# Hybrid encoder trunk: convolution steps moved between the scores and the transpositions of the prompt's second pair of heads

## Chip, cores and metric

One NeuronCore of a Trainium2 chip runs the whole program. The metric is the device time in microseconds (us) of one execution, as the median of several runs. The engines are TensorE (PE in the profile, its weight loads PEld), VectorE (DVE), ScalarE (ACT), GpSimd (POOL) and SyncE (SP), which here only issues DMAs.

## What is computed

Two batches pass through one layer with the same weights: a prompt of 256 tokens and a sample of 512, so six tiles of 128 tokens, 1024 features each. The layer is

```python
h = rmsnorm(x, norm1)
gq, gk, gv, gg, glr, dq, dk, dvv, sz, sxbc, sdt = split(h @ w_in)
x = x + concat([gla(...), diff(...), ssd(...)]) @ w_out
x = x + square(relu(rmsnorm(x, norm2) @ w_mlp1)) @ w_mlp2
```

Two of the three mixers matter here. Differential attention (diff) has four heads, each with two maps: q and k are normed over 64 features and partly rotated, and with p the softmax of the scaled scores the output is (p1 - lam p2) v, normed again. The state-space mixer (ssd) first sends 768 channels through a convolution of five taps along the tokens and silu; 512 of them are its x, 128 each its B and C:

```python
xbc = silu(conv(sxbc, conv_w, width=5) + conv_b)
```

## The kernel before

**Work and order.** The program is written in Python as one long function. A scheduler then sets the order on each engine's queue, by the dependences, by priorities and by its own idea of how long things take. `tc.high_priority()` moves what stands in it ahead in that order; `tc.issue_after(i)` keeps what stands in it behind the instruction i. On the chip each engine works its queue strictly in the order written, TensorE too, so what stands at the head and waits holds all behind it.

**Products.** All weights are float32 and are split into a high part (a rounding, ScalarE's cast, L135) and a low part (VectorE's subtraction, L136), `wh` and `wl`; a product is three matmuls (`mm3`, L97 to L101). A unit of weights is 256 columns of w_in: two loads `wr` of 512 KB, two casts, two subtractions. `wh` and `wl` have two buffers each, so a unit's cast waits for the last product of the unit before the previous one. `tm_steps` multiplies tokens by a unit (tile `tm`, 256 columns, 48 matmuls for two token tiles); `fm_unit` (L201) makes features by tokens (tile `fm`, 384 columns, 24 matmuls for one of two halves). Both, and the convolution's transpositions `xtmp`, share three accumulators of PSUM (`acc`, N_ACC = 3); all else shares the other five (`mx`).

**Norms of q and k.** `diff_in(p)` (L801) makes q and k of head pair p in two units. After each two token tiles ScalarE copies the product to `dqk` and squares it to `dsq`; VectorE sums (L817, `dss`), POOL takes the power -1/2 (`rstd_of`, L160, `drs`), VectorE scales (L819) and rotates (L824 to L827); a DMA writes `dqk` to memory. The small columns come from `small`, a ring of eight tiles of 32 columns.

**Heads.** `diff_head(p, h, 0)` (L841) reads q, k and v of one prompt head back, transposes q and k (`qT`, L866), splits them (`qs`, `ks`, `kz`), and for each of the two query tiles makes the two maps' scores (`sc`, L890 and L891), the row maximum (`dmx`, L892), the exponential with its sum (`pr`, L893), mixes the maps (`dratio`, `pr`, L894 to L896), transposes the result (`wT`, L899) and splits it (`wt`, L903 and L904). After both tiles it multiplies by v (`O`) and norms (`ss`, `ors`, `dg`, `rb`). It yields after its set-up and after each tile; `take_turns` lets the heads of a pair advance in turn.

**Convolution.** `ssd_conv` (L616) takes three units of 256 channels, in the order 2, 0, 1, and in each two times 128 channels. For each it makes both halves of the product, ScalarE copies them to `xp` (L625 to L628) and starts the sum (`zh`, L632), VectorE adds four taps (L634). `tail`, always one channel group late, does the silu (tanh on ScalarE, L199; VectorE L646 or L654), and for x transposes the result back (`xtmp`, L650; `xt`, L651).

**The stretch in question.** Behind the first mixer (gla), at about 222 us of the trace, the program has:

```python
for p in range(2):
    diff_in(p)
    take_turns(*(diff_head(p, h, 0) for h in range(2)))
xt, bcm = [None] * 4, [None] * 2
tail = ssd_conv((2, 0, 1), xt, bcm)
ssd_gate(0)
tail()
btm = ssd_btm(bcm[0])
```

`ssd_gate` makes the gate's tokens (`tm`, `sz`), `ssd_btm` transposes B (`btmp`). `er` and `ar` are the tables of decays of `ssd_chunk` (L726 to L729), which the scheduler also places in this stretch. Behind it come the states and chunks of the prompt's ssd, w_out and the MLP of the prompt with the sample's heads among them, and the MLP of the sample.

Of the kernel before, what the change touches and what calls it, by code (L numbers as in the profile page):

```python
# [11 lines left out]
F32 = mybir.dt.float32  # L12
# [31 lines left out]
def hybrid_kernel(ctx, tc, io):  # L44
# [12 lines left out]
    def nm(s):  # L57
        uid[0] += 1
        return f"{s}_{uid[0]}"
# [17 lines left out]
    d2 = tag(first, "d2", 2, 2 * (T + 32))  # L77

    def small(name, n):
        return sm.tile([P, 32], F32, tag="sm", name=nm(name))[:, :n]  # L80

    def small2(name, n):
        return sm.tile([P, 32], F32, tag="sm2", name=nm(name), bufs=3)[:, :n]

    def acc(name):
        return psa.tile([P, 512], F32, tag="acc", name=nm(name))
# [7 lines left out]
    def bc(ap, shape):  # L94
        return ap.to_broadcast(shape)

    def mm3(out, l, r, first, last):  # L97
        (lh, ll), (rh, rl) = l, r
        mm(out, lhsT=lh, rhs=rh, start=first, stop=False)  # L99
        mm(out, lhsT=lh, rhs=rl, start=False, stop=False)  # L100
        return mm(out, lhsT=ll, rhs=rh, start=False, stop=last).ins  # L101
# [55 lines left out]
    def rstd_of(out, ss, n, scale, small=small):  # L157
        ms = small("ms", n)
        dve.tensor_scalar(ms, ss, scale, EPS, op0=ALU.mult, op1=ALU.add)
        pool.tensor_tensor(out, ms, nhalf[:, :n], ALU.pow)  # L160
# [40 lines left out]
    def fm_unit(w, c, m, consume, parts):  # L201

        for ops, o, n, d in parts:
            ps = acc("fm")
            for k in range(KT):
                mm3(ps[:m, :n], (w[0][:, k, c:c + m], w[1][:, k, c:c + m]),
                    tuple(z[:, o:o + n] for z in ops[k]), k == 0, k == KT - 1)
            consume(ps[:m, :n], slice(d, d + n))

    halves_ = [(hT, 0, 384, 0), (hT, 384, 384, 384)]  # L210

# [403 lines left out]
                act.activation(decs[gs], ptb[gs, :, 4 * g:4 * g + 4, :].rearrange("p d h c -> p c d h"), AF.Exp)  # L615
        yield scr, decs, tms, ew  # L616

    def ssd_conv(us, xt, bcm):
        def conv(j):
            xp = i3("xp", n=776)  # L620

            def consume(ps, ts):
                with tc.high_priority():
                    if ts.start == 0:
                        act.copy(xp[:, 2:258], ps[:, 0:256])  # L625
                        act.copy(xp[:, 262:390], ps[:, 256:384])
                        return
                    act.copy(xp[:, 390:774], ps)  # L628
                for a in (0, 258, 774):
                    pool.memset(xp[:, a:a + (4 if a == 258 else 2)], 0.0)  # L630
                zh = i3("zh", n=772)
                act.activation(zh, xp[:, 0:772], AF.Identity, scale=half[:, j:j + 1], bias=half[:, 30 + j:31 + j])  # L632
                for k in range(1, 5):
                    dve.scalar_tensor_tensor(zh, xp[:, k:k + 772], half[:, 6 * k + j:6 * k + j + 1], zh,  # L634
                                             op0=ALU.mult, op1=ALU.add)
                tails.append((j, xp, zh))
            return consume

        tails = []

        def tail():
            j, xp, zh = tails.pop(0)
            tanh(xp[:, 0:772], zh, 1.0)
            if j < 4:
                xt[j] = v128(i3("xt"))
                dve.scalar_tensor_tensor(zh, xp[:, 0:772], 1.0, zh, op0=ALU.add, op1=ALU.mult)  # L646
                for (a, b) in SEQS:
                    pt = acc("xtmp")
                    for c in range(a, b):
                        nc.tensor.transpose(pt[:, (c - a) * P:(c - a + 1) * P], zh[:, off(c):off(c) + P], ident)  # L650
                    act.copy(xt[j][:, a:b, :], v128(pt[:, :(b - a) * P]))  # L651
            else:
                bcm[j - 4] = i3("bcm", n=772)
                dve.scalar_tensor_tensor(bcm[j - 4], xp[:, 0:772], 1.0, zh, op0=ALU.add, op1=ALU.mult)  # L654

        for u in us:
            w = in_unit(C_SX + 256 * u)
            for i in range(2):
                fm_unit(w, i * P, P, conv(2 * u + i), halves_)
                if len(tails) > 1:  # L660
                    tail()
        return tail

    def ssd_btm(bfm):
        btm = s2("btm")
# [20 lines left out]
    def hd(ap):  # L686
        return ap.rearrange("p (h d) -> p h d", d=64)
# [117 lines left out]
    def diff_in(p):  # L805

        for i, c0 in ((0, C_DQ), (1, C_DK)):
            w = in_unit(c0 + 256 * p)

            def cons(ps, t0):  # L810
                q = i3("dqk", n=512)
                with tc.high_priority():
                    act.copy(q.rearrange("p (t c) -> p t c", t=2), ps)
                sq = i3("dsq", n=512)
                act.activation(sq, q, AF.Square)
                ss, rs = small("dss", 8), small("drs", 8)
                dve.tensor_reduce(ss, hd(sq), AX.X, ALU.add)  # L817
                rstd_of(rs, ss, 8, 1.0 / 64)
                dve.tensor_tensor(hd(q), hd(q), bc(rs[:, :, None], [P, 8, 64]), ALU.mult)  # L819
                q4 = q.rearrange("p (t m d) -> p t m d", t=2, m=4)  # L820
                rab = sq[:, 0:256].rearrange("p (a t m d) -> p a t m d", a=2, t=2, m=4)
                ra, rb = rab[:, 0], rab[:, 1]
                ts = slice(t0, t0 + 2)
                dve.tensor_tensor(ra, q4[:, :, :, 0:16], bc(ropeg[:, i, 0, ts, None, :], [P, 2, 4, 16]), ALU.mult)  # L824
                dve.tensor_tensor(rb[:, :, :, 0:8], q4[:, :, :, 8:16], bc(ropeg[:, i, 1, ts, None, 0:8], [P, 2, 4, 8]), ALU.mult)
                dve.tensor_tensor(rb[:, :, :, 8:16], q4[:, :, :, 0:8], bc(ropeg[:, i, 1, ts, None, 8:16], [P, 2, 4, 8]), ALU.mult)
                dve.tensor_tensor(q4[:, :, :, 0:16], ra, rb, ALU.add)  # L827
                nc.sync.dma_start(out=(dqd, dkd)[i][p][t0 // 2], in_=q.rearrange("p (t c) -> p t c", t=2))
            tm_unit(w, cons)
        for _ in v_steps[p]:  # L830
            pass
# [6 lines left out]
            nc.sync.dma_start(out=dvd[p][t0 // 2], in_=v)  # L838
        return tm_steps(lambda: in_unit(C_DV + 256 * p), vcons)

    def diff_head(p, h, s):  # L841

        a, b = SEQS[s]
        kt = b - a
# [36 lines left out]
        for pq in range(0, kt, 2):  # L881
            wts = [[tt("wt", F32R, 512).rearrange("p (k q) -> p k q", k=2) for _ in range(kt // 2)] for _ in range(2)]
            for qi in range(2):
                tq = slice((pq + qi) * P, (pq + qi + 1) * P)
                pr = cc("pr", n=2 * nk).rearrange("p (m i) -> p m i", m=2)
                mxs, ratio = small("dmx", 2), small("dratio", 1)
                sums = allsums[:, pq + qi, :]
                for m in range(2):
                    ps = mx("sc")
                    mm(ps[:, :nk], lhsT=qs[:, m, tq], rhs=ks[:, m], start=True, stop=False)  # L890
                    mm(ps[:, :nk], lhsT=qs[:, m, tq], rhs=kl[:, m], start=False, stop=True)  # L891
                    dve.tensor_reduce(mxs[:, m:m + 1], ps[:, :nk], AX.X, ALU.max, negate=True)  # L892
                    act.activation(pr[:, m], ps[:, :nk], AF.Exp, bias=mxs[:, m:m + 1], accum_out=sums[:, m:m + 1])  # L893
                dve.reciprocal(ratio, sums[:, 1:2])  # L894
                dve.scalar_tensor_tensor(ratio, ratio, nlam, sums[:, 0:1], op0=ALU.mult, op1=ALU.mult)
                dve.scalar_tensor_tensor(pr[:, 0], pr[:, 1], ratio, pr[:, 0], op0=ALU.mult, op1=ALU.add)  # L896
                ps = mx("wT")
                for k_ in range(kt):
                    nc.tensor.transpose(ps[:, k_ * P:(k_ + 1) * P], pr[:, 0, k_ * P:(k_ + 1) * P], ident)  # L899
                cols_ = slice(qi * P, (qi + 1) * P)  # L900
                for k2 in range(kt // 2):
                    src = v128(ps[:, k2 * 256:k2 * 256 + 256])
                    act.copy(wts[0][k2][:, :, cols_], src)  # L903
                    dve.tensor_tensor(wts[1][k2][:, :, cols_], src, rd(wts[0][k2][:, :, cols_]), ALU.subtract)  # L904
                yield
            for k_ in range(kt):
                mm3(po[:, pq * P:pq * P + 256], tuple(v[:, k_, :] for v in vs),
                    tuple(w[k_ // 2][:, k_ % 2, :] for w in wts), k_ == 0, k_ == kt - 1)
# [193 lines left out]
    rope = t2("rope", n=192).rearrange("p (a t d) -> p a t d", a=2, t=NT)  # L1102
    nc.sync.dma_start(out=rope, in_=io["c_rope"])

    qk16 = small("qk16", 32).rearrange("p (a d) -> p a d", a=2)
    for i, nme in enumerate(("diff_qnorm", "diff_knorm")):
        nc.sync.dma_start(out=qk16[:, i, :], in_=bc(io[nme][0:1, 0:16], [P, 16]))
    ropeg = const.tile([P, 2, 2, NT, 16], F32, name="ropeg")
# [45 lines left out]
        for m in range(2):  # L1154
            pool.memset(rd(z[64 - 64 * m:128 - 64 * m, m]), 0.0)

    for p in range(2):
        diff_in(p)
        take_turns(*(diff_head(p, h, 0) for h in range(2)))
    xt, bcm = [None] * 4, [None] * 2  # L1160
    tail = ssd_conv((2, 0, 1), xt, bcm)
    ssd_gate(0)
    tail()
    btm = ssd_btm(bcm[0])
    st = ssd_states(dt, xt, btm, *SEQS[0], tt)
    y_ops = {}
# [272 lines left out]
```

## Time and profile before

| | |
|---|---|
| runs | 1128.51, 1130.4, 1131.89 us; median 1130.4 |
| profiled execution | 1128.8 us, its span 1127.0 us |
| busy in the span: PE, PEld | 1080.3 us (96%), 982.7 us (87%) |
| busy in the span: DVE, ACT, POOL | 806.0 us (72%), 622.2 us (55%), 126.2 us (11%) |
| mean granted clock of TensorE | 0.986 |

The span is from the first to the last instruction; 1.8 us of the execution lie around it. Busy times of PE are of overlapping matmuls: one of 384 columns is shown with 0.34 us, and the next starts 0.17 us later. A wait is shown as idle time of an engine ahead of an instruction, with the instruction that ended it.

### The profile page before, as it was taken

The page shows a single profiled execution, that of the slowest core. Times are in us where ns is not written, and L with a number is a line of the kernel's source. Part 1 is how long each engine was busy: PE and PEld are TensorE (multiplying, and loading weights), DVE is VectorE, ACT ScalarE, POOL GpSimd, SP SyncE. Part 2 cuts the span into 40 slices and gives each one's busy share as a digit, 9 for nine tenths or more (in the row PEclk, how much of TensorE's full clock was granted, in tenths as well). Part 3 has the DMA queues.
Part 4 walks back from the last instruction along what each step waited for, and adds up shares of the span by engine and source line. Part 5 has one row for each costly group of instructions (what it writes and reads, how often), then busy time and mean ns, then how long its engine had stood idle before and what let it go on. Part 6 is the DMA issues. An engine that isn't in the chain of part 4 may idle for free.

```text
span 1127.0 us, 20930 instructions
## 1 busy us (share of the span) xinstructions
PE 1080.3 (96%) x8372; PEld 982.7 (87%) x8372; DVE 806.0 (72%) x1414; ACT 622.2 (55%) x1216; POOL 126.2 (11%) x184
## 2 busy tenths in 40 slices
PE   7999999999958998899999999998999999999998
PEld 7999999999958985888878897787998998998997
DVE  6579977474787578887797786857986756756752
ACT  7487584656366237656667673525553553543541
POOL 1001012120400281010101111300000000000000
PEclk9999999999989999899999999999999999999999
DMA  6212112171424354446545558642351242342312
GB/s 203 88 42 77 40 58 89 56 225 39 149 71 127 103 194 143 130 134 194 181 128 170 178 159 276 218 133 89 97 188 59 94 133 74 94 140 67 94 38 75
DMA packets 118647, 136.49 MB, mean 121 GB/s; under 512 B 8935, under 2 KB 86789, under 8 KB 118549
## 3 DMA queue, kind: packets, MB, share of 16 engines
q1 hardware_dynamic: 118517, 135.14, 37.5%
q8 instruction: 66, 1.08, 0.4%
q14 instruction: 32, 0.26, 0.1%
q10 hardware_dynamic: 32, 0.01, 0.0%
HBM read 121.44 MB, written 13.68 MB: 120 GB/s over the span
## 4 chain that ended last, share of the span: by engine, by line
PE 76%; DVE 8%; ACT 6%; DMA 5%; POOL 2%; issue 2%; SPq 0%; ACTq 0%; DVEq 0%; POOLq 0%
PE tp L100 9%; PE tp L99 9%; PE tp L101 9%; PE X L1297 7%; PE fm L99 5%; PE fm L100 5%; PE fm L101 5%; PE tm L99 4%; PE tm L101 4%; PE tm L100 4%; PE Z L1297 4%; DMA wr<-in_w_mlp 2%; DVE wl L136 2%; DMA er<-scr 2%; PE Y L1297 2%
## 5 line engine op out<-in xcount | busy, mean ns | idle before, releaser
L136 DVE TENSOR_TENSOR wl<-wr,wh 128x1024 fp32r<-128x1024 f32 x130 | 160.2, 1246 | 54.0 <-ACT wh L135 53.2
L135 ACT CAST wh<-wr 128x1024 fp32r<-128x1024 f32 x138 | 141.6, 1049 | 96.6 <-DMA wr<-in_w_mlp 49.3
L99 PE MATMUL tm<-wh,hTh 128*128 128x256 f32 x576 | 166.3, 289 | 3.6 <-ACT xp L628 3.5
L101 PE MATMUL tm<-wh,hTl 128*128 128x256 f32 x576 | 165.1, 287 | 0.0
L100 PE MATMUL tm<-wl,hTh 128*128 128x256 f32 x576 | 163.4, 284 | 0.0
L99 PEld LDWEIGHTS tm<-wh,hTh 128*128 128x128 f32 x576 | 109.9, 191 | 5.6 <-ACT xp L628 3.7
L100 PEld LDWEIGHTS tm<-wl,hTh 128*128 128x128 f32 x576 | 109.9, 191 | 0.4 <-DVE wl L136 0.2
L101 PEld LDWEIGHTS tm<-wh,hTl 128*128 128x128 f32 x576 | 110.0, 191 | 0.1
L1390 DVE TENSOR_TENSOR xres<-tp,xres 128x512 f32<-128x512 f32 x56 | 38.6, 690 | 55.4 <-PE tp L101 54.7
L99 PE MATMUL fm<-h,wh 128*128 128x256 f32 x256 | 73.0, 287 | 1.9 <-ACT relu L1002 1.9
L100 PE MATMUL fm<-h,wh 128*128 128x256 f32 x256 | 73.2, 287 | 0.0
L101 PE MATMUL fm<-h,wl 128*128 128x256 f32 x256 | 72.4, 286 | 0.5 <-DVE wl L136 0.5
L99 PE MATMUL fm<-hTh,wh 128*128 128x384 f32 x160 | 54.4, 340 | 2.2 <-ACT xp L628 2.2
L100 PE MATMUL fm<-hTl,wh 128*128 128x384 f32 x160 | 54.1, 338 | 0.0
L101 PE MATMUL fm<-hTh,wl 128*128 128x384 f32 x160 | 53.9, 337 | 0.0
L956 DVE TENSOR_TENSOR xres<-tp,xres 128x512 f32<-128x512 f32 x60 | 40.3, 683 | 17.4 <-PE tp L101 17.3
L99 PEld LDWEIGHTS fm<-h,wh 128*128 128x128 f32 x256 | 49.5, 194 | 2.6 <-ACT relu L1002 2.1
L100 PE MATMUL tp<-wl,u 128*128 128x512 f32 x128 | 50.9, 398 | 0.5 <-DVE wl L136 0.5
L101 PE MATMUL tp<-wh,u 128*128 128x512 f32 x128 | 50.6, 395 | 0.0
L99 PE MATMUL tp<-wh,u 128*128 128x512 f32 x128 | 49.8, 400 | 0.6 <-ACT wh L135 0.6
L100 PEld LDWEIGHTS fm<-h,wh 128*128 128x128 f32 x256 | 49.5, 193 | 0.6
L101 PEld LDWEIGHTS fm<-h,wl 128*128 128x128 f32 x256 | 49.3, 194 | 0.9 <-DVE wl L136 0.7
(429 smaller groups left out, 3079.9 us busy)
## 6 DMA issues: line engine op xcount, KB each, us to landing
wr<-in_w_mlp SPq DMA_DIRECT2D x100, 512.0 KB
wr<-in_w_in SPq DMA_DIRECT2D x30, 512.0 KB
wb<-in_w_mlp SPq DMA_DIRECT2D x28, 512.0 KB
wr<-in_w_out SPq DMA_DIRECT2D x24, 512.0 KB
ar<-scr SPq DMA_DIRECT2D x6, 512.0 KB
er<-scr SPq DMA_DIRECT2D x6, 512.0 KB
x<-in_x_sample SPq DMA_DIRECT2D x4, 512.0 KB
wr<-in_w_in SPq DMA_DIRECT2D x8, 256.0 KB
```

Of the source, the lines that this page charges most:

```text
L99: mm(out, lhsT=lh, rhs=rh, start=first, stop=False)
L100: mm(out, lhsT=lh, rhs=rl, start=False, stop=False)
L101: return mm(out, lhsT=ll, rhs=rh, start=False, stop=last).ins
L135: act.copy(hi, raw)
L136: dve.tensor_tensor(lo, raw, rd(hi), ALU.subtract)
L956: dve.tensor_tensor(xres[t][:, cs], ps, xres[t][:, cs], ALU.add)
L1297: mm(out, lhsT=a[l][:, k, c], rhs=b[r][:, k, :], start=first and j == k == z == 0, stop=j == 1 and k == 3 and z == 2, skip_group_check=True)
L1390: dve.tensor_tensor(xres[t][:, cs], ps, xres[t][:, cs], ALU.add)
```

## The change

Four edits.

1. `ssd_conv` becomes a generator: it yields after each half of each product, with that half's last matmul, and gets the list into which it puts its `tail`.
2. `diff_head` may be given `between`. Then, for each query tile, behind the mixing of the maps it yields, calls `between(h)`, and puts the transposition `wT` behind the instructions that this returns.
3. The program takes the first four steps of the convolution (its first unit) ahead of the second pair's heads; head 0 of that pair asks for two steps for each query tile, head 1 for one; what is left follows the heads.
4. In `diff_in` the square, the sum, the power, the scaling and the rotation stand under high priority, with a ring `small8` of nine tiles of 8 columns of their own; `small` shrinks to 16 columns, and `qk16`, its one user of 32, becomes a constant.

```diff
     def small(name, n):
-        return sm.tile([P, 32], F32, tag="sm", name=nm(name))[:, :n]
+        return sm.tile([P, 16], F32, tag="sm", name=nm(name))[:, :n]
...
+    def small8(name, n):
+        return sm.tile([P, 8], F32, tag="sm8", name=nm(name), bufs=9)[:, :n]
...
+        tails.append(tail)
         for u in us:
             w = in_unit(C_SX + 256 * u)
             for i in range(2):
-                fm_unit(w, i * P, P, conv(2 * u + i), halves_)
-                if len(tails) > 1:
+                consume = conv(2 * u + i)
+                yield fm_unit(w, i * P, P, consume, halves_[:1])
+                last = fm_unit(w, i * P, P, consume, halves_[1:])
+                if len(waiting) > 1:
                     tail()
-        return tail
+                yield last
...
-                act.activation(sq, q, AF.Square)
-                ss, rs = small("dss", 8), small("drs", 8)
-                dve.tensor_reduce(ss, hd(sq), AX.X, ALU.add)
-                rstd_of(rs, ss, 8, 1.0 / 64)
-                dve.tensor_tensor(hd(q), hd(q), bc(rs[:, :, None], [P, 8, 64]), ALU.mult)
+                ss, rs = small8("dss", 8), small8("drs", 8)
...
+                with tc.high_priority():
+                    act.activation(sq, q, AF.Square)
+                    dve.tensor_reduce(ss, hd(sq), AX.X, ALU.add)
+                    rstd_of(rs, ss, 8, 1.0 / 64, small8)
+                    dve.tensor_tensor(hd(q), hd(q), bc(rs[:, :, None], [P, 8, 64]), ALU.mult)
...
-                ps = mx("wT")
-                for k_ in range(kt):
-                    nc.tensor.transpose(ps[:, k_ * P:(k_ + 1) * P], pr[:, 0, k_ * P:(k_ + 1) * P], ident)
+                with ExitStack() as order:
+                    if between is not None:
+                        yield
+                        for last in between(h):
+                            order.enter_context(tc.issue_after(last))
+                    ps = mx("wT")
+                    for k_ in range(kt):
+                        nc.tensor.transpose(ps[:, k_ * P:(k_ + 1) * P], pr[:, 0, k_ * P:(k_ + 1) * P], ident)
...
-    for p in range(2):
-        diff_in(p)
-        take_turns(*(diff_head(p, h, 0) for h in range(2)))
-    xt, bcm = [None] * 4, [None] * 2
-    tail = ssd_conv((2, 0, 1), xt, bcm)
+    xt, bcm, tails = [None] * 4, [None] * 2, []
+    steps = ssd_conv((2, 0, 1), xt, bcm, tails)
+    diff_in(0)
+    take_turns(*(diff_head(0, h, 0) for h in range(2)))
+    diff_in(1)
+    for _ in range(4):
+        next(steps)
+    take_turns(*(diff_head(1, h, 0, lambda h: [next(steps) for _ in range(2 - h)]) for h in range(2)))
+    for _ in steps:
+        pass
     ssd_gate(0)
-    tail()
+    tails[0]()
```

What the scheduler makes of it is seen in the queues. Line numbers of the changed program are some 3 to 20 higher. **TensorE, at the first wT of the second pair, before:** `fm` are convolution products, `sc_530` and `sc_531` the scores of head 0, `sc_540` and `sc_541` those of head 1.

```order
L101 MATMUL fm_591_4718<-hTh_24_137,wl_581_4615 128x384
L890 MATMUL sc_531_4347<-ks_511_4290,qs_510_4289 128x256
L891 MATMUL sc_531_4347<-kz0_3254,qs_510_4289 128x256
L899 MATMUL wT_532_4355<-ident_94,pr_527_4339 128x128 x2
L890 MATMUL sc_540_4367<-ks_520_4318,qs_519_4317 128x256
L891 MATMUL sc_540_4367<-kz1_3258,qs_519_4317 128x256
L890 MATMUL sc_541_4372<-ks_520_4318,qs_519_4317 128x256
L891 MATMUL sc_541_4372<-kz1_3258,qs_519_4317 128x256
L650 MATMUL xtmp_594_4756<-ident_94,zh_587_4681 128x128 x2
```

**The same place in the change,** the last rows ahead of wT and the first behind it; `sc_552`, the last score of head 1, stands 29 rows ahead of wT.

```order
L102 MATMUL fm_576_4660<-hTh_24_137,wh_553_4514 128x384
L103 MATMUL fm_576_4660<-hTl_25_138,wh_553_4514 128x384
L104 MATMUL fm_576_4660<-hTh_24_137,wl_554_4515 128x384
L914 MATMUL wT_562_4590<-ident_94,pr_539_4478 128x128 x2
L655 MATMUL xtmp_579_4698<-ident_94,zh_560_4581 128x128 x2
L655 MATMUL xtmp_580_4702<-ident_94,zh_560_4581 128x128 x4
L102 MATMUL fm_586_4719<-hTh_10_123,wh_581_4708 128x384
```

Both heads' scores now stand ahead of the first wT, with the whole of `fm_576` and four rows of `fm_564` between, and the transpositions `xtmp` directly behind it.

**VectorE, the end of the same wait, in the change** (`wl_614` is the low part of the gate's weights):

```order
L904 RECIPROCAL dratio_541_4480<-dsum_536_4475 128x1
L902 TENSOR_REDUCE dmx_549_4499<-sc_551_4501 128x1
L902 TENSOR_REDUCE dmx_549_4499<-sc_552_4506 128x1
L639 SCALAR_TENSOR_TENSOR zh_560_4581<-xp_557_4524,half_644,zh_560_4581 128x772
L905 SCALAR_TENSOR_TENSOR dratio_541_4480<-dratio_541_4480,nlam_812,dsum_536_4475 128x1
L639 SCALAR_TENSOR_TENSOR zh_560_4581<-xp_557_4524,half_644,zh_560_4581 128x772
L906 SCALAR_TENSOR_TENSOR pr_539_4478<-pr_539_4478,dratio_541_4480 128x256
L139 TENSOR_TENSOR wl_614_4929<-wr_615_4930,wh_613_4928 128x1024
L139 TENSOR_TENSOR wl_614_4929<-wr_616_4934,wh_613_4928 128x1024
L651 SCALAR_TENSOR_TENSOR zh_560_4581<-xp_557_4524,zh_560_4581 128x772
```

Before, the two `wl` of the same weights stood ahead of pr; now they stand between pr and the last step of the `zh` that `xtmp_579` transposes.

**VectorE, one step of the first pair's heads, in the change** (`dqk_471` is a normed tile of the second pair's q):

```order
L902 TENSOR_REDUCE dmx_431_3759<-sc_434_3766 128x1
L832 TENSOR_TENSOR dqk_471_3993<-dqk_471_3993,drs_474_3997 128x512
L904 RECIPROCAL dratio_432_3760<-dsum_427_3755 128x1
L833 TENSOR_TENSOR dsq_472_3995<-dqk_471_3993,ropeg_798 128x128
L834 TENSOR_TENSOR dsq_472_3995<-dqk_471_3993,ropeg_798 128x8x8
L835 TENSOR_TENSOR dsq_472_3995<-dqk_471_3993,ropeg_798 128x8x8
L905 SCALAR_TENSOR_TENSOR dratio_432_3760<-dratio_432_3760,nlam_812,dsum_427_3755 128x1
L836 TENSOR_TENSOR dqk_471_3993<-dsq_472_3995 128x8x16
L906 SCALAR_TENSOR_TENSOR pr_430_3758<-pr_430_3758,dratio_432_3760 128x256
L139 TENSOR_TENSOR wl_505_4280<-wr_506_4281,wh_504_4279 128x1024
```

Before, no scaling or rotation of the second pair's norms stood among the first pair's heads; now one norm's stands within each step.

## Rows read from the trace of the kernel before

**Rows 1.** Waits of TensorE, 225 to 380 us: us in total, times, longest.
```profile
PE wT L899 <- DVE pr L896: 11.1, 1, 11.1
PE tm L99 <- ACT xp L628: 3.5, 1, 3.5
PE fm L99 <- ACT xp L628: 2.2, 1, 2.2
```

**Rows 2.** Timeline of TensorE where the waits end: start, us, operation, [idle before, releaser].
```profile
295.17 0.44 PE L99 MATMUL fm<-hTh,wh 128*128 128x384 f32 x1 [2.18 <-ACT xp L628]
...
329.24 0.66 PE L899 MATMUL wT<-ident,pr 128*128 128x128 f32 x2 [11.09 <-DVE pr L896]
...
356.12 0.39 PE L99 MATMUL tm<-wh,hTh 128*128 128x256 f32 x1 [3.50 <-ACT xp L628]
```

**Rows 3.** Stretches: length, busy us of PE, PEld, DVE, ACT, POOL, granted clock, DMA.
```profile
245.00:285.00 40.00, 39.76 (x324) 39.50 (x323) 19.88 (x50) 23.18 (x51) 2.33 (x2) 1.00 0.28 84
294.40:329.20 34.80, 22.74 (x132) 22.18 (x132) 34.32 (x68) 21.56 (x43) 8.73 (x22) 0.90 0.46 144
294.00:296.00 2.00, 0.83 (x5) 0.83 (x6) 2.00 (x8) 0.93 (x3) 2.00 (x5) 1.00 0.44 162
328.00:332.00 4.00, 2.76 (x13) 2.79 (x14) 3.97 (x8) 1.67 (x5) 0.00 (x0) 0.50 0.02 6
356.00:360.00 4.00, 3.88 (x20) 3.89 (x21) 3.86 (x7) 3.83 (x9) 0.00 (x0) 0.57 0.67 235
```

**Rows 4.** Groups on VectorE, 225 to 378 us: count, busy us, mean ns, idle before.
```profile
L634 DVE SCALAR_TENSOR_TENSOR zh<-xp,half,zh 128x772 f32<-128x772 f32 x24 | 24.3, 1015 | 0.2
L136 DVE TENSOR_TENSOR wl<-wr,wh 128x1024 fp32r<-128x1024 f32 x14 | 16.7, 1218 | 2.0 <-ACT wh L135 1.9
L819 DVE TENSOR_TENSOR dqk<-dqk,drs 128x512 f32<-128x512 f32 x10 | 6.8, 684 | 1.1 <-POOL drs L160 1.1
L817 DVE TENSOR_REDUCE dss<-dsq 128x8 f32<-128x512 f32 x10 | 6.8, 678 | 2.2 <-ACT dsq L815 2.2
L892 DVE TENSOR_REDUCE dmx<-sc 128x1 f32<-128x256 f32 x16 | 6.6, 420 | 8.9 <-PE sc L891 8.6
L896 DVE SCALAR_TENSOR_TENSOR pr<-pr,dratio 128x256 f32<-128x256 f32 x8 | 3.9, 483 | 0.2
L646 DVE SCALAR_TENSOR_TENSOR zh<-xp,zh 128x772 f32<-128x772 f32 x4 | 3.8, 958 | 0.5 <-ACT xp L199 0.4
L824 DVE TENSOR_TENSOR dsq<-dqk,ropeg 128x128 f32<-128x128 f32 x12 | 3.4, 286 | 0.1
```

**Rows 5.** Timeline of VectorE, the first and last dss after 288 us.
```profile
288.56 0.68 DVE L817 TENSOR_REDUCE dss<-dsq 128x8 f32<-128x512 f32 x1
...
299.61 0.67 DVE L817 TENSOR_REDUCE dss<-dsq 128x8 f32<-128x512 f32 x1
```

**Rows 6.** Timeline of TensorE, 296.6 to 301.4 us.
```profile
296.85 0.34 PE L99 MATMUL fm<-hTh,wh 128*128 128x384 f32 x1
...
301.19 0.34 PE L100 MATMUL fm<-hTl,wh 128*128 128x384 f32 x1
...
301.36 0.27 PE L866 MATMUL qT<-ident,dqkv 128*128 128x128 f32 x1
```

**Rows 7.** Groups on ScalarE, 294.4 to 356.2 us.
```profile
L135 ACT CAST wh<-wr 128x1024 fp32r<-128x1024 f32 x6 | 6.0, 1044 | 1.8 <-PE fm L100 1.8
L726 ACT ACTIVATE er<-er,tms 128x128 f32<-128x128 f32 x16 | 5.1, 397 | 0.0
L199 ACT ACTIVATE xp<-zh 128x772 f32<-128x772 f32 x5 | 4.2, 847 | 4.4 <-DVE zh L634 4.4
L893 ACT ACTIVATE pr<-sc,dmx 128x256 f32<-128x256 f32 x8 | 3.8, 484 | 0.4 <-DVE dmx L892 0.3
L628 ACT COPY xp<-fm 128x384 f32<-128x384 f32 x6 | 2.9, 480 | 2.7 <-PE fm L101 2.7
```

**Rows 8.** Tile drs on POOL, whole span: ns min/median/max, starts.
```profile
L160 POOL TENSOR_TENSOR drs<-ms,nhalf x12: 1637/1639/2951, 219.5 to 303.4; 128x8 f32<-128x8 f32 x12
```

More of the change, by code (lines that the diff above doesn't have):

```diff
@@ L205, in fm_unit @@
             for k in range(KT):
-                mm3(ps[:m, :n], (w[0][:, k, c:c + m], w[1][:, k, c:c + m]),
-                    tuple(z[:, o:o + n] for z in ops[k]), k == 0, k == KT - 1)
+                last = mm3(ps[:m, :n], (w[0][:, k, c:c + m], w[1][:, k, c:c + m]),
+                           tuple(z[:, o:o + n] for z in ops[k]), k == 0, k == KT - 1)
             consume(ps[:m, :n], slice(d, d + n))
+        return last
     halves_ = [(hT, 0, 384, 0), (hT, 384, 384, 384)]
@@ L616, in ssd_dt, with ssd_conv @@
         yield scr, decs, tms, ew
-    def ssd_conv(us, xt, bcm):
+    def ssd_conv(us, xt, bcm, tails):
         def conv(j):
@@ L635, in consume @@
                                              op0=ALU.mult, op1=ALU.add)
-                tails.append((j, xp, zh))
+                waiting.append((j, xp, zh))
             return consume
-        tails = []
+        waiting = []
         def tail():
-            j, xp, zh = tails.pop(0)
+            j, xp, zh = waiting.pop(0)
             tanh(xp[:, 0:772], zh, 1.0)
@@ L823, in cons @@
                 ts = slice(t0, t0 + 2)
[L824 to L827, printed above, removed]
+                with tc.high_priority():
[3 more added lines that the diff above has]
+                    dve.tensor_tensor(hd(q), hd(q), bc(rs[:, :, None], [P, 8, 64]), ALU.mult)
+                    dve.tensor_tensor(ra, q4[:, :, :, 0:16], bc(ropeg[:, i, 0, ts, None, :], [P, 2, 4, 16]), ALU.mult)
+                    dve.tensor_tensor(rb[:, :, :, 0:8], q4[:, :, :, 8:16], bc(ropeg[:, i, 1, ts, None, 0:8], [P, 2, 4, 8]), ALU.mult)
+                    dve.tensor_tensor(rb[:, :, :, 8:16], q4[:, :, :, 0:8], bc(ropeg[:, i, 1, ts, None, 8:16], [P, 2, 4, 8]), ALU.mult)
+                    dve.tensor_tensor(q4[:, :, :, 0:16], ra, rb, ALU.add)
                 nc.sync.dma_start(out=(dqd, dkd)[i][p][t0 // 2], in_=q.rearrange("p (t c) -> p t c", t=2))
@@ L839, in diff_v, with diff_head @@
         return tm_steps(lambda: in_unit(C_DV + 256 * p), vcons)
-    def diff_head(p, h, s):
+    def diff_head(p, h, s, between=None):
         a, b = SEQS[s]
@@ L1103, in hybrid_kernel @@
     nc.sync.dma_start(out=rope, in_=io["c_rope"])
-    qk16 = small("qk16", 32).rearrange("p (a d) -> p a d", a=2)
+    qk16 = const.tile([P, 32], F32, name="qk16").rearrange("p (a d) -> p a d", a=2)
     for i, nme in enumerate(("diff_qnorm", "diff_knorm")):
```

## Prediction

> **What bounds the kernel now.** I read four views, from the whole to the place. The first is the list of TensorE's waits in the stretch 225 to 380 us, where the change lies [rows 1]: three entries matter, 11.1 us in which the transposition of the second pair's softmax (wT) waits for VectorE's pr, and 3.5 and 2.2 us in which a product waits for ScalarE's copy out of the accumulator (xp). The timeline gives their places [rows 2]: products resume at 295.17, 329.24 and 356.12 us. Outside these waits TensorE is full there, so it is TensorE's queue that sets the end, and every microsecond of waiting there is one of the total. The table of stretches says why wT waits [rows 3]: from 245 to 285 us VectorE works 19.88 of 40.00 us, from 294.4 to 329.2 us it works 34.32 of 34.80. VectorE is idle where TensorE is fed and full where TensorE starves. The same table shows the granted clock: 0.50 after the 11.09 us wait, 0.57 after the 3.50 us wait, 1.00 after the 2.18 us wait. [...]
>
> So the three waits cost 11.09 + 2.18 + 3.50 = 16.8 us and the clock 2 x 1.7 = 3.4 us: **20.2 us** is the most the change can win.
>
> **The change, part by part.** No product, transposition or norm is added or dropped; the sum is about where queues stand.
>
> *Norms ahead.* One norm is a sum of squares (0.678), a scaling (0.684) and a rotation in four instructions (0.286 the longest, some 1.0 in all): 2.4 us of VectorE [rows 4]. In the trace all six sums of squares of the second pair's norms lie between 288.56 and 299.61 us [rows 5], and their scalings and rotations follow them one by one, so 6 x 2.4 = 14 us of the full stretch are norms. In the new order all six stand ahead of the first convolution step on VectorE, between the first heads' operations, into the 20 us that VectorE idles from 245 to 285 [rows 3]: nothing, as long as the first heads' softmax is not held up (a rival below). The 2.18 us wait goes with this: ScalarE's copy of the first convolution product was held because its target's buffer still belonged to a norm's tile; now the norms are through some 10 us before. Gain 2.18.
>
> *Convolution between scores and wT.* In the order of before wT stands directly behind the last score. Now 28 products stand between (4 + 24), and counted from the pair's first q/k transposition to wT TensorE has 89 products of 384 columns. Products start 0.1735 us apart (296.85 to 301.19 us, 25 steps; 4.34 / 25) [rows 6]. To see whether VectorE comes first I start both engines where the last product of the first convolution unit ends (call it T), since ScalarE's cast of the next weights waits for that. TensorE from T to wT: 4 x 24 = 96 products, 16.7 us, and 8 transpositions, 8 scores and one rb, some 2: T + 18.8. VectorE can begin when ScalarE has cast half a weight block, T + 1.0 [rows 7]. Its queue up to pr is 2 wl (2 x 1.218), 8 zh (1.015), 2 bcm (0.95, as L646), 8 qs and kz (as pr, 0.48), 4 dmx (0.42), 3 splits and one product of dmx's size, and pr 0.48 with its two columns (0.4) [rows 4], together 20.5; neighbours overlap by some 0.08 each (zh starts 0.93 apart), 2 off, 1 back for places where it waits for ScalarE: 19.5. pr is ready at T + 20.5, **wT waits 1.7 us**. Bounds: 0.7 if VectorE never waits, 7.3 from the rival below.
>
> *Behind wT.* The convolution's transpositions (xtmp) follow at once on TensorE. Their operand is the last zh step, and in VectorE's new order two wl stand between pr and it: 2 x 1.218 + 0.958 [rows 4] = 3.4, less 0.25 of wT itself: **3.1 us**. Nothing covers it. The second head's pr is behind that too, but TensorE has 17 products (2.9 us) by then: covered.
>
> *Where the 3.50 us wait was.* From the end of the third unit's first channel ScalarE has a copy 0.48, an affine step of 1.04 (as the cast), 16 er (5.1) and casts, copies and an exponential of some 4, 10.5 in all [rows 7]; TensorE has 48 products and small things, 10.1. Then tanh 0.847 and the last zh step (0.958) stand before the next transpositions, and two casts (2 x 1.044) and a copy (0.48) before the gate's first product may have its accumulator [rows 7]. I get 0.4 + 1.5 + 0.7 = **2.6 us** in three pieces. The trace's own 3.50 is the upper bound, 0.7 the lower (the copy alone).
>
> *Clock.* The waits of 1.7 and 3.1 us have only wT, 0.25 us, between them. [...]
>
> *Other queues.* POOL's powers (drs, 1.64 us [rows 8]) move with the norms; the xp memsets stand behind them and nobody waits. On SP the six writes and the reads of q, k, v move forward with the norms; the write of the first head's result (mixa) now stands ahead of the reads of the second head's k and v and waits for its sq, about 10 us before the transpositions that need them: covered. The casts of the gate's weights on ScalarE stand ahead of the second head's exponentials and wait for the last product of their buffer; the single spare pr buffer makes those exponentials wait for wT anyway: covered. The small tiles of 16 columns, the nine of 8 and qk16 as a constant cost nothing: rings of buffers that no row shows as a wait.
>
> *Sum.* 20.2 won; 1.7 + 3.1 + 2.6 = 7.4 of new waits and 1.7 of clock: 20.2 - 9.1 = 11.1. After the last transposition of this stretch (378 us) the order is the same on all engines but for a few swapped rows among the sample's heads, so the gain is carried to the end. The profiled execution took 1128.8 us, giving 1117.7; it is 1.6 below the median of the runs, from which it would be 1119.3. I say **1118**.
>
> **The rivals.**
>
> *All waits vanish.* VectorE's overlap is better than I took, wT finds pr, ScalarE's queue drains in time. For: the new stretch is TensorE's by 18.8 against 19.5, a near tie. Against: the two wl ahead of xtmp. The full 20.2: 1108.6.
>
> *VectorE as slow as before.* From the second pair's first q transposition (301.36 [rows 6]) to wT (329.24 [rows 2]) the trace took 27.9 us; without the norm work that was in it (two scalings and two rotations, 3.4) 24.5. My walk gives 18.9 for it (7 products and rb lie between T and that transposition, so T + 1.6 to T + 20.5). If the rest is as dense as it was, wT waits 5.6 longer, 7.3 in all: gain 5.5, 1123.3 (1120 to 1126). For: VectorE was full. Against: four of the zh steps of that stretch have moved ahead.
>
> *The wait only moves.* VectorE stays full until wT, whatever stands between: the reading if the norms did not leave. The gain is under 3.4 us: 1125.4 to 1130. Against: the new order has the norms elsewhere.
>
> *Slower: the norms starve the first heads.* Where: VectorE's queue between the first heads' scores and their four wT, which cost TensorE nothing before. Between them TensorE has 48 products of 256 columns, 48 x 0.1157 = 5.6 us (two thirds of 0.1735). The chain from score to pr is about 2.5 (dmx 0.42, exponential 0.484, pr 0.48 and small ones [rows 4, 7]); in the new order about 1.6 us of norm stands in it, 4.1: slack 1.5. It decides when more than 1.5 us of further work falls in front: a held power (2.951 instead of 1.639 [rows 8], 1.3) does not quite do it, two wl (2.4) behind schedule do. With both and a whole norm more (2.4) the chain is 10.2, each of the four wT waits 4.6, and with four stretches of low clock (6.8) that is 25.2: 1128.8 - 11.1 + 25.2 = 1143. It is slower than before once these waits are over 11.1 in all. [...]
>
> **How the numbers follow.** Forecast 0.60, its own range 1113 to 1123 (waits and clock at their bounds). All waits vanish 0.14, VectorE as slow 0.13, the wait only moves 0.08, slower 0.05. A measurement of this kernel can tell some 0.3%, 3.4 us, from no change. Faster is 0.60 + 0.14 + 0.13 = 0.87, same 0.08, slower 0.05. The range 1109 to 1126 holds the forecast and nearly all of the two other faster cases: about 0.83.
>
> **What would show it.** In the changed profile: no wait of 11 us at wT, one of 1 to 3 us there and one of about 3 us at xtmp directly behind, released by VectorE's zh; a wait of 1 to 3 us at the gate's first product; the granted clock at 1.00 but for one or two stretches of low clock as long as the two read above; VectorE well above half busy from 245 to 285; no wait at the first pair's wT. I am wrong if TensorE waits at the first heads' wT or if wT of the second pair still waits over 6 us.

## The result, and the profile after

| | before | changed | ratio, 95% interval |
|---|---|---|---|
| median, first chip | 1130.31 us | 1121.34 us (1119.85 to 1122.57) | 0.9917 (0.9902 to 0.9933) |
| median, second chip | 1132.49 us | 1119.66 us (1119.42 to 1121.88) | 0.9899 (0.9881 to 0.9916) |
| profiled execution, its span | 1128.8, 1127.0 us | 1119.85, 1118.1 us | |
| mean granted clock | 0.986 | 0.990 | |

The change makes the kernel 0.8 to 1.0 % faster. The forecast was 1118, the range 1109 to 1126. Two of all executions took far longer than the others of their kernel, 2130.61 us (the profiled one of priority_only, its mean granted clock shown as 1.00) and 2691.25 us (one of tail_later_no_priority), and no median here holds them.

The waits of TensorE in the changed kernel, 225 to 380 us (us in total, times, longest), which answer to [rows 1]:

```profile
PE xtmp L655 <- DVE zh L651: 2.7, 1, 2.7
PE xtmp L655 <- DVE oes L931: 1.3, 1, 1.3
PE wT L914 <- DVE pr L906: 1.1, 1, 1.1
```

The 11.09 us at wT are 1.1, the 2.18 us are gone, and the 3.50 us at the gate's first product are 1.3 at the xtmp ahead of it. New are 2.7 at the xtmp directly behind wT. Before, the scores that stand behind that wT in TensorE's queue began at 329.55 us, behind it, though the last of their operands (kz) was ready at 325.25. The stretches (length, busy us of PE, PEld, DVE, ACT, POOL, granted clock, DMA share, GB/s), to be read beside [rows 3]:

```profile
245.00:285.00 40.00, 39.76 (x328) 39.56 (x327) 31.52 (x85) 26.21 (x57) 10.58 (x10) 1.00 0.38 120
294.40:329.20 34.80, 30.98 (x172) 30.32 (x171) 29.22 (x47) 22.01 (x47) 1.19 (x13) 0.90 0.26 77
322.00:328.00 6.00, 4.39 (x16) 4.39 (x17) 5.79 (x10) 3.29 (x9) 0.00 (x0) 0.50 0.60 179
346.00:352.00 6.00, 4.69 (x38) 4.49 (x36) 5.69 (x14) 6.00 (x10) 1.36 (x1) 1.00 0.32 85
```

VectorE's work has moved from the second row (34.32 to 29.22) into the first (19.88 to 31.52). From 225 to 380 us the granted clock is at 0.50 once, at 322 to 328 us, and it is 1.00 around the 1.3 us wait (346 to 352 us). The second pair's first and last sums of squares, which answer to [rows 5], stand at:

```profile
255.57 0.69 DVE L830 TENSOR_REDUCE dss<-dsq 128x8 f32<-128x512 f32 x1
...
285.40 0.68 DVE L830 TENSOR_REDUCE dss<-dsq 128x8 f32<-128x512 f32 x1
```

And TensorE at the first two waits, which answers to [rows 2] (start, us, operation, idle before and what ended it):

```profile
320.46 0.44 PE L914 MATMUL wT<-ident,pr 128*128 128x128 f32 x2 [1.11 <-DVE pr L906]
323.61 1.54 PE L655 MATMUL xtmp<-ident,zh 128*128 128x128 f32 x6 [2.71 <-DVE zh L651]
324.80 0.67 PE L102 MATMUL fm<-hTh,wh 128*128 128x384 f32 x1
325.27 0.52 PE L103 MATMUL fm<-hTl,wh 128*128 128x384 f32 x1
325.59 0.52 PE L104 MATMUL fm<-hTh,wl 128*128 128x384 f32 x1
```

Behind the second wait a product starts every 0.32 us, not every 0.17 [rows 6].

### The profile page after: what moved, and what is told of

Same layout as the page of the kernel before. It is cut to its first block, busy times and chain, and to the rows that moved or that the text cites. A ratio compares the mean times of both kernels' runs of the same rounds, so it can differ in the third digit from the quotient of the medians.

```text
span 1118.1 us, 20921 instructions
## 1 busy us (share of the span) xinstructions
PE 1083.0 (97%) x8372; PEld 984.9 (88%) x8372; DVE 805.6 (72%) x1414; ACT 621.3 (56%) x1216; POOL 123.3 (11%) x184
## 4 chain that ended last, share of the span: by engine, by line
PE 75%; DVE 9%; ACT 6%; DMA 5%; issue 2%; POOL 2%; SPq 0%; DVEq 0%; ACTq 0%; POOLq 0%
PE tp L102 9%; PE tp L103 9%; PE tp L104 9%; PE X L1317 7%; PE fm L102 5%; PE fm L103 5%; PE fm L104 5%; PE tm L102 4%; PE tm L104 4%; PE tm L103 4%; PE Z L1317 4%; DVE wl L139 2%; PE Y L1317 2%; DMA wr<-in_w_mlp 2%; DMA er<-scr 1%
```

## Experiments

Twelve runs followed; changed_again and priority_again are the changed kernel and priority_only once more. Ratios are to runs of the kernel before on the same chip.

| kernel | median us | ratio, 95% interval |
|---|---|---|
| priority_again | 1132.78 | one execution, no interval |
| edits123_only | 1132.19 | 1.0001 (0.9985 to 1.0017) |
| priority_only | 1131.14 | 0.9995 (0.9979 to 1.0010) |
| ring_only | 1126.75 | 0.9960 (0.9944 to 0.9975) |
| edit4_only | 1124.34 | 0.9943 (0.9926 to 0.9961) |
| gate_weights_later | 1123.63 | 0.9923 (0.9907 to 0.9939) |
| no_priority | 1121.67 | 0.9904 (0.9885 to 0.9924) |
| changed_again | 1119.66 | 0.9899 (0.9881 to 0.9916) |
| ring_tail_later | 1118.68 | 0.9892 (0.9871 to 0.9913) |
| tail_later_no_priority | 1116.79 | 0.9872 (0.9849 to 0.9896) |
| tail_later | 1115.46 | 0.9857 (0.9838 to 0.9876) |
| weights_in_place | 1112.83 | 0.9827 (0.9802 to 0.9852) |

### Which edit brings it

**edits123_only** takes edit 4 back (the operations that stood under the priority, the ring's definition, the 32 columns of `small` and the old place of qk16 are not shown):

```diff
-                ss, rs = small8("dss", 8), small8("drs", 8)
...
+                ss, rs = small("dss", 8), small("drs", 8)
...
-                with tc.high_priority():
...
```

> The changed kernel with edit 4 taken back: convolution steps between scores and wT, norms as before in the old ring of small and without priority. Theory A: the norms stay in the full stretch, TensorE has only four more score products ahead of wT, wT waits 9 to 11.5 us, time 1126 to 1131. Theory B: wT waits under 5 us, time 1120 to 1124.

No gain at all. TensorE's three largest waits in 225 to 380 us, and the clock behind them:

```profile
PE wT L910 <- DVE pr L902: 4.2, 1, 4.2
PE sc L896 <- ACT ks L881: 3.2, 1, 3.2
PE sc L897 <- DVE kz L882: 3.1, 1, 3.1
```
```profile
324.00:328.00 4.00, 0.58 (x1) 0.28 (x1) 3.94 (x6) 3.46 (x10) 0.17 (x3) 0.54 0.60 154
328.00:332.00 4.00, 0.58 (x1) 0.29 (x1) 3.94 (x9) 0.85 (x1) 0.00 (x0) 0.50 0.46 141
332.00:336.00 4.00, 3.08 (x12) 2.72 (x13) 3.86 (x8) 2.37 (x8) 0.00 (x0) 0.50 0.03 6
```

Theory A missed the place: wT waits 4.2, but two scores ahead of it wait 3.2 and 3.1 for the splits of q and k. VectorE is as full as before there (fourth column, 3.94 of 4.00). The wait of 11.1 came in three pieces, 10.5 in all. Theory A's cause stands; the median, 1132.19, is 1.2 above the range that it gave and 8 above theory B's.

**edit4_only** is the kernel before with edit 4 alone, as the diff of the change has it.

> The kernel before with edit 4 alone: the norms' small columns in a ring of nine of their own, and the norms under high priority; the convolution stands as before behind the heads in the program, and no step is placed between scores and wT by hand. Theory A (the gain comes from the norms' leaving VectorE's full stretch, and the scheduler then fills TensorE by itself): some 1120 us, within 3 of the changed kernel, wT of the second pair waits under 2 us, and the convolution product takes no 2.2 us wait. Theory B (the hand-placed convolution steps bring it, the norms only their 2.2): 1126 to 1129, wT still waits over 7 us.

7.1 us, more than half of the gain. The median, 1124.34, lies between the two theories' times; the waits at wT and at the convolution product decide for A, and two others are left:

```profile
PE tm L102 <- ACT xp L631: 3.4, 1, 3.4
PE xtmp L653 <- DVE zh L649: 3.1, 1, 3.1
PE wT L903 <- DVE pr L900: 0.9, 1, 0.9
```

Once the norms were out of the way the scheduler by itself put 29 products between the last score of the first head and wT, where the kernel before had none. What it lacks of the changed kernel is the last place: the gate's first product still waits 3.4, as before [rows 1]. As I read the queues, the heads' second scores and exponentials stand late there; with `between` their transpositions stand ahead of the last channel's products, and 1.3 are left. So edits 1 to 3 are worth nothing alone, and some 3 to 5 us on top of edit 4 (3.0 against the first chip's median of the changed kernel, where the intervals overlap, 4.7 against the second's, where they don't).

**ring_only and priority_only** split edit 4: the first has the ring and no `tc.high_priority()`, the second the priority and `small`.

> The kernel before with only the ring of nine tiles of 8 columns for the norms (and qk16 as a constant, small of 16 columns): no high priority, no convolution between. If the ring is what held the norms back (they shared eight tiles of small with the heads' columns): the second pair's norms stand among the first pair's heads on VectorE as in the changed kernel, and the time is 1119 to 1123. If the high priority is what moves them: 1127 to 1131, wT waits 8 to 11 us.

> The kernel before with only the high priority on the norms, in the old ring of small. If the ring holds them, the norms stay behind 288 us on VectorE and the time stays over 1126 (some microsecond may be won or lost by the other order of a few instructions there); if priority alone frees them, 1119 to 1123.

> priority_only once more, for a profile of an execution at the usual clock. Theory (the old ring of small holds the norms, whatever their priority): the sums of squares of the second pair lie between 287 and 301 us on VectorE as in the kernel before, VectorE is under 60 % busy from 245 to 285, and TensorE waits 10 us or more in all between 225 and 380. Rival: the norms lie among the first pair's heads and something else gave the time back.

The ring alone gives 4.7 us, the priority alone nothing. The median of ring_only, 1126.75, lies between the times of its two theories, 0.25 below the one for the priority; the norms' place decides it, for the ring: there the second pair's sums of squares stand from 255.58 to 287.98 us. The waits of the priority alone are read from priority_again: xtmp waits 9.3, fm 2.7. VectorE there, with the second pair's first and last sum of squares:

```profile
245.00:285.00 40.00, 39.88 (x327) 39.63 (x327) 20.78 (x52) 23.73 (x52) 2.34 (x2) 1.00 0.29 82
```
```profile
289.22 0.68 DVE L822 TENSOR_REDUCE dss<-dsq 128x8 f32<-128x512 f32 x1
...
298.17 0.67 DVE L822 TENSOR_REDUCE dss<-dsq 128x8 f32<-128x512 f32 x1
```

With the old ring the norms stay where they were [rows 5], whatever their priority. In ring_only VectorE works 29.74 of the 40.00 us and wT does not wait at all; xtmp waits 4.7 and the gate's product 3.4.

**no_priority** is the changed kernel with the ring and without the priority.

> The changed kernel with the norms' ring of nine but without their high priority. With the ring alone, on the kernel before, 4.7 us were won, with ring and priority 7.1. Theory A (the priority has a share of its own, about 2.4): 1122 to 1125, and TensorE waits more than the 2.7 at xtmp, or at another place. Rival (with both scores ahead of wT the priority has nothing left to do): within 1 us of the changed kernel, 1119 to 1122.

The rival: 1121.67 against 1119.66, waits of 2.7, 1.3 and 1.2, the same as with it. Between edit4_only and ring_only, and between tail_later and tail_later_no_priority, the intervals overlap too. No single pair shows a gain by the priority that is more than the scatter. But in all three the kernel with the priority has the lower ratio, by 0.0005 to 0.0017, so a gain of up to some 2 us on top of the ring is neither shown nor excluded.

### The waits that are left

**gate_weights_later** puts the gate's weights behind the tanh and the last zh step of the first xtmp, which `silus[0]` keeps (how it gets them is not shown):

```diff
-    ssd_gate(0)
+    with tc.issue_after(silus[0][0].ins), tc.issue_after(silus[0][1].ins):
+        ssd_gate(0)
```

> The changed kernel with the first gate unit's weights (two casts on ScalarE, two wl on VectorE) queued behind the tanh and the last zh step of the channel group that the first xtmp transposes. My step said that two wl between pr and zh make the xtmp wait. Theory A (they alone): with 2.4 less on VectorE the 2.7 wait falls to under 0.6. Theory B (ScalarE's tanh is late as well: it ended 0.3 before VectorE was free, and now an affine step of 1.0 stands ahead of it): the wait falls only to 1.6 to 2.2, time 1119 to 1121.

Theory B for the wait. In the changed kernel ScalarE and VectorE stand so at that place:

```profile
319.21 1.99 ACT L138 CAST wh<-wr 128x1024 fp32r<-128x1024 f32 x2 [2.30 <-PE fm L103]
...
321.48 0.85 ACT L202 ACTIVATE xp<-zh 128x772 f32<-128x772 f32 x1
```
```profile
319.94 0.47 DVE L906 SCALAR_TENSOR_TENSOR pr<-pr,dratio 128x256 f32<-128x256 f32 x1
320.33 2.35 DVE L139 TENSOR_TENSOR wl<-wr,wh 128x1024 fp32r<-128x1024 f32 x2
322.60 0.95 DVE L651 SCALAR_TENSOR_TENSOR zh<-xp,zh 128x772 f32<-128x772 f32 x1
```

The two wl (2.35) stand ahead of zh, as I said, but zh could not have begun before the tanh ended, at 322.33: the same weights' casts hold ScalarE for 1.99. With the weights out of the way an affine step takes the casts' place, and the wait falls only to 2.06. What the weights were moved past is paid at the gate, where the first product now waits:

```profile
PE tm L102 <- ACT xp L635: 3.0, 1, 3.0
PE xtmp L658 <- DVE zh L654: 2.1, 1, 2.1
```

1123.6, outside both theories' times: neither of them had named that queue. It is not the whole account: the profiled execution is 1.6 us longer than that of changed_again, the median 4.0.

**tail_later** leaves the engines' work alone and gives TensorE 24 more products ahead of wT and xtmp:

```diff
-                yield fm_unit(w, i * P, P, consume, halves_[:1])
-                last = fm_unit(w, i * P, P, consume, halves_[1:])
+                last = fm_unit(w, i * P, P, consume, halves_[:1])
                 if len(waiting) > 1:
                     tail()
                 yield last
+                yield fm_unit(w, i * P, P, consume, halves_[1:])
+        tail()
```

> The changed kernel, with each channel group's tail (tanh, last zh step, transpositions xtmp) called half a product later: TensorE has 24 more products of 384 columns (4.2 us) ahead of the first wT and xtmp of the second pair. Theory A (these two waits are VectorE's and ScalarE's queue finishing late, and 4.2 us of products cover both): the waits of 1.1 and 2.7 are gone and with them the stretch of low clock behind them (some 2.5), 6.3 in all: 1113 to 1117. Rival (VectorE is full there, so the wait only moves to the next transposition or score): a new wait of 2 to 4 us behind, 1118 to 1122.

Theory A, 1115.46: better than the changed kernel on the same chip, with intervals that don't meet. The waits (225 to 380 us) and the clock:

```profile
PE tm L102 <- ACT xp L633: 1.2, 1, 1.2
PE qT L877 <- DMA dqkv<-dkd: 1.0, 1, 1.0
...
PE xtmp L655 <- DVE zh L651: 0.3, 1, 0.3
```
```profile
318.00:330.00 12.00, 11.72 (x70) 11.47 (x69) 10.75 (x19) 7.74 (x16) 0.00 (x0) 1.00 0.30 88
```

The clock stays at 1.00. Of the 6.3 us some 4.2 reach the end: part is given back further on, where the transposition of the ssd's result waits for a norm that runs on VectorE, POOL and ScalarE and not on TensorE. There tail_later waits 1.05 and 3.75, the changed kernel 1.82:

```profile
407.19 0.44 PE L788 MATMUL yT<-ident,y 128*128 128x128 f32 x2 [1.05 <-ACT y L784]
...
420.78 0.48 PE L788 MATMUL yT<-ident,y 128*128 128x128 f32 x1 [3.75 <-ACT y L784]
```

**ring_tail_later** is the kernel before with two edits, the ring as in ring_only and the tails as in tail_later.

> The kernel before with two edits only: the norms' ring of nine (as in ring_only) and the tails called half a product later (as in tail_later); nothing is placed by hand between scores and wT, and the norms have no high priority. Theory (what counts is the ring and products enough ahead of wT and xtmp; the hand-placed steps of edits 1 to 3 are one way to it): the first wT has 16 products ahead of it that it had not in ring_only, the 4.7 us wait at xtmp is gone, and 1116 to 1120 comes out. Rival (the placed steps are needed: the second head's scores come late without them): the wait at the gate's first product stays at 3 us or more with a stretch of low clock, 1121 to 1125.

The theory: 1118.68, with no wait above 0.9 in the stretch. Two small edits give what all four of the change give, within the noise.

**tail_later_no_priority.**

> tail_later without the norms' high priority. In no_priority the priority was worth nothing within 1 us of noise; with the same theory this one equals tail_later, 1114 to 1117 (ratio to it within 0.3 %). Rival (with the waits gone the first heads' wT come into reach of the norms): 1117 to 1120, waits at the first pair's wT.

The theory: 1116.79, waits as in tail_later but for the q transposition's (0.3 for 1.0), none at the first pair's wT. The intervals overlap: as above, not to be told from no difference.

### Where the rest of the difference between the profiles lies

**changed_again.**

> The changed kernel once more, unaltered, on the chip of the next three: its other executions. Theory: the 2.4 us that its profiled execution lost before 100 us are the first stretch of low clock, whose end differs from execution to execution and has nothing to do with the change; then the end of that stretch lies elsewhere this time (15 to 18 us), and the waits of 225 to 380 us are the same within 0.3. Rival: the change itself brings them (another place of the small columns, another order of loads); then it ends at 18.2 again. Time 1119 to 1123.

Before 100 us the changed kernel's profiled execution falls 2.4 us behind. The first part is a slow start: the program's first products start 0.21 us apart, as products of 256 columns do in the kernel before where the granted clock is shown as 0.50 (356.51 to 359.72 us, 15 steps), though it is shown as 1.00 here, and at some point they start 0.12 apart. That point, before and after:

```profile
14.89 0.36 PE L99 MATMUL tm<-wh,hTh 128*128 128x256 f32 x1
15.09 0.28 PE L100 MATMUL tm<-wl,hTh 128*128 128x256 f32 x1
```
```profile
17.51 0.41 PE L102 MATMUL tm<-wh,hTh 128*128 128x256 f32 x1
17.72 0.41 PE L103 MATMUL tm<-wl,hTh 128*128 128x256 f32 x1
...
18.20 0.28 PE L102 MATMUL tm<-wh,hTh 128*128 128x256 f32 x1
```

Before, the slow start ended at 15.1 us, in the changed kernel at 18.2, which makes 1.5 us by 34 us. In changed_again it ended at 15.3, so the theory holds for this part; in edits123_only it ended at 10.5, in weights_in_place at 17.6.

Another part came back the same in both: between `cols_ps` and `tms` TensorE has 117 products of 384 columns that nothing holds up, and they take 20.78 us in every kernel with edit 4's constant and 20.41 in every kernel without. **weights_in_place** tests the reason, on top of tail_later:

```diff
-    qk16 = const.tile([P, 32], F32, name="qk16").rearrange("p (a d) -> p a d", a=2)
+    qk16 = sm.tile([P, 32], F32, tag="qk16", name="qk16", bufs=1).rearrange("p (a d) -> p a d", a=2)
```

> tail_later, with qk16 in the pool of small columns instead of among the constants; all queues keep their order. As a constant, qk16 lies ahead of the weight buffers and moved wh, wl and wr by 128 bytes of each partition. In all kernels with that constant so far the 117 convolution products between cols_ps and tms near 43 us took 20.78 us, in the three without it 20.41, in every profiled execution. Theory (the weights' place sets the pace of products of 384 columns): 20.41 again, some 0.003 us for each of about 480 such products, 1.5 us in all: 1113 to 1115, of which a median can hardly tell; the stretch in the trace decides. Rival (the ring of nine or the other tiles, moved by 96 bytes, do it): 20.78, no gain.

The theory, by the stretch. First the changed kernel's two tiles that bound the products, then those of weights_in_place: 64.58 - 43.80 = 20.78 and 63.82 - 43.42 = 20.40.

```profile
43.80 0.27 PE L1089 MATMUL cols_ps<-ident,rows 128*128 128x128 f32 x1
64.58 0.55 PE L600 MATMUL tms<-ident,stk 112*128 112x112 f32 x4
```
```profile
43.42 0.27 PE L1090 MATMUL cols_ps<-ident,rows 128*128 128x128 f32 x1
63.82 0.74 PE L600 MATMUL tms<-ident,stk 112*128 112x112 f32 x6
```

The queues of weights_in_place and tail_later are row for row the same; by the program's allocation wh begins at byte 23680 of a partition with the constant ahead of it and at 23552 without. At 0.37 per 117 products, some 480 such products in the kernel cost an estimated 1.5 us. The median, 1112.83, is the lowest of all, but its interval overlaps tail_later's and both profiled spans are 1112.3 us: the pace of the 117 products is shown, a gain in the whole time is not.

## Why the prediction was right, step by step

Direction, size and the main mechanism held, with one step wrong and some luck in the sum. 9.0 us were won by the medians of the first chip and 12.8 by those of the second; the forecast lies 12.4 below the median shown.

- **Norms ahead: right, and it is the key.** All six sums of squares of the second norms stand from 255.57 to 285.40, and the 2.18 us wait went with them. But I costed the small tiles and qk16 at nothing, as rings "that no row shows as a wait". That step failed twice. The ring is what moves the norms (4.7 us alone, where the priority alone shows none): it shows in no wait, because the scheduler had already ordered around it. And qk16 as a constant moves the weights, an estimated 1.5 us in the whole kernel.
- **wT: 1.7 forecast, 1.11 measured.** The near tie of VectorE and TensorE was there.
- **Behind wT: 3.1 forecast, 2.71 measured, by half the reason.** I named the two wl; ScalarE's two casts of the same weights hold the tanh until 322.33, and without these weights in the way 2.06 of the wait were left in gate_weights_later.
- **The gate's place: 2.6 in three pieces forecast, 1.31 in one measured.** The profile names VectorE's oes as what ended it; the zh step that xtmp transposes ended at 348.15, just ahead of it. The gate's first product itself waits no longer.
- **Clock: 1.7 forecast, about 2.3 measured.** No run shows 1.7 for the two near waits together. The changed kernel lost about 2.3 behind them: from 324.80 to 328.47 TensorE makes 11 steps in 3.67 us, 1.7 more than at 0.177, and the transpositions lose 0.5. In changed_again the mean granted clock from 322 to 328 us was 0.72 instead of 0.50, and TensorE was busy for 5.38 of the 6.00 us instead of 4.39. For a stretch of low clock behind one wait 1.7 is about right: before, 18 products of 256 columns took 3.76 us from 356.12 to 359.88, 1.7 more than at the 0.117 of such products at a clock of 1.00. That two near waits count together was a guess, and stays one. gate_weights_later is in line with it: 1.12 and 2.06 with wT between brought the clock to 0.50, while 2.18 alone had left it at 1.00 [rows 2, 3]. But in priority_again a wait of 2.66 with no other near it lowered the clock too, and in the kernel before so did one of 1.93, so the length of a wait does not settle it by itself. First the two waits of gate_weights_later and the clock behind them, then the single ones of priority_again and of the kernel before:

```profile
320.59 0.44 PE L917 MATMUL wT<-ident,pr 128*128 128x128 f32 x2 [1.12 <-DVE pr L909]
323.09 0.47 PE L658 MATMUL xtmp<-ident,zh 128*128 128x128 f32 x1 [2.06 <-DVE zh L654]
```
```profile
323.00:325.00 2.00, 1.91 (x8) 1.91 (x9) 2.00 (x3) 2.00 (x7) 0.00 (x0) 0.50 0.04 8
```
```profile
296.32 0.69 PE L99 MATMUL fm<-hTh,wh 128*128 128x384 f32 x1 [2.66 <-ACT xp L628]
```
```profile
298.00:300.00 2.00, 2.00 (x7) 2.00 (x7) 2.00 (x9) 1.06 (x3) 1.66 (x4) 0.50 0.53 178
```
```profile
587.16 0.39 PE L99 MATMUL fm<-h,wh 128*128 128x256 f32 x1 [1.93 <-ACT relu L1002]
```
```profile
589.00:591.00 2.00, 2.00 (x12) 2.00 (x11) 2.00 (x6) 1.05 (x1) 0.00 (x0) 0.50 0.14 26
```

- **The sum.** From the first convolution product to the product behind btmp, before and after:

```profile
278.29 0.34 PE L99 MATMUL fm<-hTh,wh 128*128 128x384 f32 x1
...
378.63 0.39 PE L99 MATMUL tm<-wh,hTh 128*128 128x256 f32 x1
```
```profile
281.02 0.34 PE L102 MATMUL fm<-hTh,wh 128*128 128x384 f32 x1
...
369.73 0.39 PE L102 MATMUL tm<-wh,hTh 128*128 128x256 f32 x1
```

  100.34 against 88.71: 11.6 won, where I had 11.1. Three errors nearly cancel in this, which is luck: 2.3 less of waits, against 0.6 more of clock and 0.9 (288 products at 0.0031) of the weights' place; 0.3 are left over. The span shows 8.9, because the changed kernel comes 2.73 late to the start: some 1.5 from the slow start, 0.6 from the weights' place (192 products), some 0.6 that I don't place, a wait of 0.24 at a score (252.72 us) among it.
- **The rivals.** "All waits vanish" fell by the wait I gave against it. "VectorE as slow as before" and "the wait only moves" fell with 1.1 at wT. "Slower" fell: the first pair's four wT stand without a wait. Its price rested in part on a power of 2.951 us instead of 1.639 among the heads; that one would come there was an estimate of mine. None did: all ten powers from 225 to 300 us of the changed kernel took 1.64 us, with VectorE 79 % busy from 245 to 285 (31.52 of 40.00). What made the power of 2.951 us before [rows 8] so long is not shown: it began at 298.23, 0.02 us behind the start of a zh step of 1.01. Nor did a pr slow down beside one of the ten: at 258.27 us it took its usual 0.48 [rows 4] within this power:

```profile
257.40 1.64 POOL L163 TENSOR_TENSOR drs<-ms,nhalf 128x8 f32<-128x8 f32 x1 [4.08 <-DVE ms L162]
```

## What to carry to other kernels

Where an engine is idle in one stretch and full in the next, ask first what keeps the work from moving ahead: here a ring of small columns did, which no view of waits shows, and priority alone did nothing against it. A wait of one engine on two full ones was cheaper to cover with work of its own (half a product unit later, 4.2 us: 1115.46 in tail_later) than by reordering the full ones, where the moved work was paid elsewhere (1123.63 in gate_weights_later). And a new constant may move every buffer behind it, here by 128 bytes with 20.78 us for 20.41: compare the pace of a long run of equal products before and after.

## What was not expected of the hardware

- A shift of the weight buffers by 128 bytes of a partition changes the pace of the 384-column products: 117 of them took 20.78 us with the buffers at the one place and 20.40 to 20.41 at the other, in all of thirteen profiled executions. Why is open: the place was moved in one step only, and with it wl and wr.
- The slow start of the program (products 0.21 us apart, the granted clock shown as 1.00) ended at 10.5 (edits123_only), 15.1 (before), 15.3, 17.6 (weights_in_place) and 18.2 us; between the two of the changed kernel (18.2 and 15.3) that is worth some 1.5 us.
- Behind the waits at wT and xtmp (1.1 and 2.7 us) the clock was low for different lengths: the mean granted clock from 322 to 328 us was 0.50 in one execution of the changed kernel and 0.72 in the other, which was 1.0 us ahead at `cols_ps` (42.78 for 43.80 us).
- A single wait of 2.66 us (priority_again) and one of 1.93 us (before, 587.16 us) lowered the clock to 0.50, one of 2.18 us left it at 1.00 (before, 295.17 us).
